# Four weight chunks of a two-layer decoder kernel split by Pool's queue one layer ahead, first convolution taps on ScalarE, statistics over wider pieces

## The chip, the cores and the metric

One NeuronCore of a Trainium2 chip runs the whole kernel. Its engines are TensorE (PE in the rows), VectorE (DVE), ScalarE (ACT), GpSimd (POOL, here called Pool) and SyncE (SP), each with an instruction queue of its own that it works off in order; an instruction that waits holds up what is queued behind it. DMAs are issued from the queues of SP and Pool here. The metric is the device time of one execution, in microseconds (us), the median of several runs.

## The reference

Two residual layers over x of 512 tokens by 1024 channels, in float32. Cut to what matters:

```python
def fox_moba_layer(x, norm_g, w_in, b_f, ..., w_out):           # layer 0
    proj = rms_norm(x, norm_g) @ w_in       # FoX q,k,v | forget logits | MoBA q,k,v | gate
    out_a = fox_attention(qa, ka, va, logf) # 8 heads: logits + c[q] - c[k], causal, softmax
    out_b = moba_attention(qb, kb, vb)      # 8 heads: top-3 key blocks + own causal block
    mix = jnp.concatenate([out_a, out_b], axis=2).reshape(B, S, MIX_WIDTH)
    return x + (mix * jax.nn.silu(gate)) @ w_out

def conformer_conv_layer(x, norm_g, w_in, conv_w, conv_b, ln_g, ln_b, w_out):   # layer 1
    val, glu_gate, z = jnp.split(rms_norm(x, norm_g) @ w_in, 3, axis=-1)
    u = val * jax.nn.sigmoid(glu_gate)
    u = causal_depthwise_conv(u, conv_w) + conv_b        # 31 taps along the tokens
    u = jax.nn.silu(layer_norm(u, ln_g, ln_b)) * jax.nn.silu(z)
    return x + u @ w_out
```

## The kernel before

**Weights.** All weights come in 36 chunks of 1 MB (128 partitions by 2048 numbers). To keep the accuracy of float32 each matrix is written as a rounded part `hi` and a remainder `lo`, and a product is three matmuls (L361 for the token-major form, L370 to L372 for the channel-major one). Chunks 0 to 15 are layer 0's input projection, 16 to 19 its output projection, 20 to 27 the value and gate halves of layer 1's GLU, 28 to 31 its z path, 32 to 35 its output projection (used in the order 33, 34, 32, 35).

**How a chunk becomes two parts.** SP fetches it into one of two staging buffers `wst` (L152). `split_w` makes `hi` as a rounded copy on ScalarE (L173) or by a casting DMA issued by Pool (L169, chunks in `CAST`). The remainder is a subtraction on VectorE or Pool (L177), or, for the chunks in `DMAS` (all from 20 on), a copy of the negated chunk on ScalarE (L175) to which a DMA issued by Pool adds the chunk itself (L179). The parts live in rings: `whi` and `wlo` with two buffers each ("main"), `wx` with four, and for chunk 32 ("late") a tile of its own, with its `hi` fetched later by Pool (L1051). `ahead` calls the split of the next chunk and the fetch of one more, so a staging buffer that is not yet read through holds up the fetches behind it on SP.

**Layer 0.** The dense work is a generator of 56 units over chunks 0 to 15; the attention of eight pairs of heads (four MoBA, then four FoX) advances it with `advance`, so that dense matmuls stand between the attention's. For FoX, Pool adds bias and mask to each tile's row of biases (L518, 32 tiles, two `cb` buffers), VectorE adds that to the scores and takes row maxima (L522), ScalarE makes the exponentials `p` (L523), TensorE transposes them (L526) and multiplies them with the values (L603) in PSUM bank "o", and VectorE divides into the slot of `ot` (L608). The slots 0 to 3 of `ot` belong to the four FoX pairs. Pool also computes the reciprocal roots of q and k (L396).

**Layer 1.** For each of eight channel tiles TensorE makes value and gate, ScalarE and VectorE make `u`, and the convolution's 31 taps are shared: VectorE does some (L766, accumulating in a PSUM bank `s`; the first tap, L763, goes to a tile `first` in SBUF), ScalarE makes products `tm` of the others (L775, six buffers) and Pool adds them up in `pacc` (L776). L783 adds both sums. Then TensorE transposes (L796), VectorE takes statistics (L798) and ScalarE copies to `ctok` (L799). The last two channel tiles, 6 and 7, go through in two halves of 256 tokens. `norm_stats` joins the statistics (L903, L904) and Pool takes the reciprocal root `lnr` (L905); `norm_cols` (L911) normalises `ctok`, TensorE transposes it back (L922), ScalarE (L928) and VectorE (L933) make the product with z, and L936 and L939 split it for the last matmuls.

**What sets the order.** A scheduler orders each engine's queue from the program and its own estimates, except the last stretch from the transposes of channel tile 6 on: there PE, DVE, ACT and POOL have the order written out by hand, with tables saying how many convolution steps stand between the others.

## Time and profile before

| | |
|---|---|
| median of 3 runs | 522.47 us (522.46 to 522.81) |
| the profiled execution | 522.39 us, of it 520.6 us span |
| TensorE busy | 503.7 us, 97% of the span |
| VectorE busy | 373.0 us, 72% |
| ScalarE busy | 329.1 us, 63% |
| Pool busy | 232.6 us, 45% |
| chain that ended last | PE 70%, DMA 8%, POOL 7%, ACT 6%, DVE 4%, issue 3% |

A row of the profile names an engine, a line of the kernel and what is written from what. Shares of busy time are means over stages: layer 0's projections and attention up to about 256 us, its output projection up to about 282, layer 1's projections with the convolution up to about 440, the convolution's end with the normalisation up to about 490, and the last matmuls. The chain of waits is followed back from the last instruction through what released each step.

### The profile page before, as it was taken

To read this page: it belongs to the slowest core of one execution; us is meant where nothing else is said; L and a number is where in the kernel's file an instruction comes from. 1 tells how busy PE (TensorE), PEld (TensorE's weight loads), DVE (VectorE), ACT (ScalarE), POOL (GpSimd) and SP (SyncE) were. 2 spreads that over 40 slices of the span, in tenths; PEclk is the share of its full clock that TensorE was granted. 3 is DMA by queue.
4 is the path that set the end of the run, shared out by engine and by line. 5 is a ranking of instruction groups with operands and counts; after the bars stand their busy time and mean duration, and the time that the engine had idled before them with its cause. 6 is when DMAs were issued, how large, how long until landed. Compare 5 with 4: busy or idle time off the path is not lost.

```text
span 520.6 us, 9754 instructions
## 1 busy us (share of the span) xinstructions
PE 503.7 (97%) x3694; PEld 459.9 (88%) x3694; DVE 373.0 (72%) x788; ACT 329.1 (63%) x668; POOL 232.6 (45%) x255
## 2 busy tenths in 40 slices
PE   8999999999999999999999999999999999769997
PEld 4999998987889988788789999999999888548997
DVE  7745677676465577596685256999999997868741
ACT  4945678777645775576384735998676765377230
POOL 5264852020422233223101113879988985687200
PEclk9999999999999999999999999999999999989999
DMA  8742222302122242402219668488999799962111
GB/s 293 318 145 81 84 81 83 102 24 83 61 102 94 82 111 99 144 14 108 102 52 395 130 205 242 82 211 286 235 306 259 212 270 305 262 170 105 41 51 42
DMA packets 16566, 79.05 MB, mean 152 GB/s; under 512 B 1988, under 2 KB 4352, under 8 KB 8712
## 3 DMA queue, kind: packets, MB, share of 16 engines
q1 hardware_dynamic: 12632, 51.08, 27.1%
q0 software_dynamic: 3744, 27.26, 22.0%
q8 instruction: 29, 0.48, 0.4%
q10 hardware_dynamic: 144, 0.09, 0.1%
q14 instruction: 17, 0.14, 0.1%
HBM read 50.07 MB, written 2.14 MB: 100 GB/s over the span
## 4 chain that ended last, share of the span: by engine, by line
PE 70%; DMA 8%; POOL 7%; ACT 6%; DVE 4%; issue 3%; SPq 0%; POOLq 0%; ACTq 0%
PE mm L361 29%; POOL pacc L776 6%; PE mm L370 6%; PE mm L371 6%; PE mm L372 6%; DMA wst<-in_w_dram 5%; PE st L361 4%; PE o L603 3%; PE tp L526 3%; PE o L361 2%; PE s L510 2%; PE s L512 2%; DMA wlo<-wst 1%; DMA xt<-in_xt_dram 1%; PE s L361 1%
## 5 line engine op out<-in xcount | busy, mean ns | idle before, releaser
L776 POOL TENSOR_TENSOR pacc<-pacc,tm 128x256 f32<-128x256 f32 (+1 forms) x125 | 120.7, 986 | 15.8 <-ACT tm L775 10.1
L766 DVE SCALAR_TENSOR_TENSOR s<-u,parts,s 128x256 f32<-128x256 f32 (+1 forms) x211 | 108.1, 569 | 0.5
L361 PE MATMUL mm<-wlo,hhi 128*128 128x256 f32 (+1 forms) x352 | 98.7, 287 | 0.8 <-DVE wlo L177 0.5
L361 PE MATMUL mm<-whi,hhi 128*128 128x256 f32 (+1 forms) x352 | 98.4, 287 | 0.0
L361 PE MATMUL mm<-whi,hlo 128*128 128x256 f32 (+1 forms) x352 | 98.3, 286 | 0.0
L775 ACT ACTIVATE tm<-u,parts 128x256 f32<-128x256 f32 (+1 forms) x125 | 66.2, 571 | 14.5 <-POOL pacc L776 14.0
L361 PEld LDWEIGHTS mm<-wlo,hhi 128*128 128x128 f32 x352 | 65.8, 190 | 2.0 <-DVE wlo L177 0.8
L361 PEld LDWEIGHTS mm<-whi,hhi 128*128 128x128 f32 x352 | 65.6, 189 | 0.7 <-issue 0.2
L361 PEld LDWEIGHTS mm<-whi,hlo 128*128 128x128 f32 x352 | 65.9, 190 | 0.2
L177 POOL TENSOR_TENSOR wlo<-wst,whi 128x512 fp32r<-128x512 f32 (+1 forms) x22 | 31.0, 1423 | 57.4 <-ACT whi L173 57.4
L173 ACT ACTIVATE whi<-wst 128x512 fp32r<-128x512 f32 (+2 forms) x77 | 49.4, 707 | 5.9 <-DMA wst<-in_w_dram 2.7
L518 POOL TENSOR_TENSOR cb<-cb,mask 128x128 f32<-128x128 f32 x32 | 15.5, 490 | 80.7 <-DVE nm L522 46.2
L523 ACT ACTIVATE p<-p,nm 128x128 f32<-128x128 f32 (+3 forms) x64 | 35.7, 559 | 24.1 <-DVE nm L522 23.6
L177 DVE TENSOR_TENSOR wlo<-wst,whi 128x512 fp32r<-128x512 f32 (+1 forms) x50 | 39.8, 830 | 9.0 <-PE o L361 7.1
L370 PE MATMUL mm<-nhi,wx 128*128 128x256 f32 (+1 forms) x104 | 33.0, 318 | 0.0
L371 PE MATMUL mm<-nlo,wx 128*128 128x256 f32 (+1 forms) x104 | 32.2, 309 | 0.0
L372 PE MATMUL mm<-nhi,wx 128*128 128x256 f32 (+1 forms) x104 | 31.9, 307 | 0.0
L371 PE MATMUL mm<-nlo,whi 128*128 128x256 f32 (+1 forms) x104 | 31.8, 307 | 0.0
L372 PE MATMUL mm<-nhi,wlo 128*128 128x256 f32 (+1 forms) x104 | 31.7, 306 | 0.0
L370 PE MATMUL mm<-nhi,whi 128*128 128x256 f32 (+1 forms) x104 | 31.7, 307 | 0.0
L526 PE MATMUL tp<-identf,p 128*128 128x128 f32 x160 | 28.4, 275 | 1.1 <-ACT p L523 0.7
L396 POOL TENSOR_TENSOR rq<-vq,mhalf 128x16 f32<-128x16 f32 x8 | 26.2, 3272 | 6.2 <-DVE vq L394 6.1
(292 smaller groups left out, 1436.3 us busy)
## 6 DMA issues: line engine op xcount, KB each, us to landing
wst<-in_w_dram SPq DMA_DIRECT2D x33, 1024.0 KB, 5.0
wx<-wst POOLq DMA_DIRECT2D x13, 1024.0 KB, 7.2
wlo<-wst POOLq DMA_DIRECT2D x8, 1024.0 KB, 8.4
whi<-wst POOLq DMA_DIRECT2D x3, 1024.0 KB, 4.5
wst<-in_w_dram SPq DMA_DIRECT2D x2, 1040.0 KB
xs<-in_x_dram SPq DMA_DIRECT2D x4, 512.0 KB, 10.3
...
```

The costliest lines, as they stand in the source:

```text
L173: A.activation(hi[:, ks], st[:, ks], AF.Copy)
L177: (V if eng is G and parts == 4 and k % 4 and V0 else eng).tensor_tensor(lo[:, ks], st[:, ks], hi[:, ks].bitcast(F32), op=ALU.subtract)
L361: T.matmul(po, a[:, k, ts], b[:, k, :n], start=first and i == 0, stop=last and i == len(prods) - 1)
L370: T.matmul(po, whi[:, k, cs], a, start=k == 0, stop=False)
L371: T.matmul(po, whi[:, k, cs], b, start=False, stop=False)
L372: T.matmul(po, wlo[:, k, cs], a, start=False, stop=k == KC - 1)
L396: G.tensor_tensor(r, v, mhalf[:, :16].rearrange("p (t h) -> p t h", t=NT), op=ALU.pow)
L523: A.activation(p[:, :w], p[:, :w], AF.Exp, bias=nm, scale=-1.0, accum_out=sm[:, h, t:t + 1])
L526: T.transpose(tp[:, j * P:(j + 1) * P], p[:, j * P:(j + 1) * P], identf)
L766: V.scalar_tensor_tensor(acc[:, o], v, w, first[0][:, :n] if i == 1 else acc[:, o], op0=ALU.mult, op1=ALU.add)
L775: A.activation(tm[:, :n], v, AF.Copy, scale=w)
L776: G.tensor_tensor(pacc[:, o], pacc[:, o], tm[:, :n], op=ALU.add)
```

## The change

Three edits.

**Chunks 30 to 33 (`PRE`) are split in layer 0.** Each is taken in four quarters. For a quarter, Pool's queue issues two DMAs from memory, the plain one into `st` and a casting one into `hi`; in the following step Pool subtracts the one from the other (128 by 512) and issues two DMAs of 256 KB that write both parts to a tile `pre` in device memory. Even quarters use the slots 0 and 1 of `ot` as buffers, odd ones 2 and 3, before the FoX pairs write there. A step is called from `advance` when the count of dense units reaches an entry of `UNITS`, and its first instruction waits for ScalarE's emptying of the newest dense unit (`unit`). In layer 1 SP fetches the finished parts straight into their rings, and neither `wst`, ScalarE nor Pool has to do with these four chunks. All in all 64 DMAs and 16 subtractions are added on Pool's queue in layer 0; four fetches into `wst`, four copies on ScalarE (three L175, one L160), three casting and four accumulating DMAs and one fetch on Pool's queue go from layer 1. Chunks 34 and 35 keep the old way.

**The first tap** is made by ScalarE, with bias and scale, straight into VectorE's PSUM bank. The tile `first` goes.

**Statistics.** For channel tiles 0 to 3 they are taken once, over 512 channels of `ctok`, for 4 and 5 over 256; 6 and 7 stay as they were. So four sets are joined instead of eight.

```diff
-DMAS = (20, 21, 22, 23, 24, 25, 26, 27, 28, 29, 30, 31, 32, 33, 34, 35)
+DMAS = (20, 21, 22, 23, 24, 25, 26, 27, 28, 29, 34, 35)
...
-CAST = (22, 26, 27, 28, 30, 31, 33, 34, 35)
+CAST = (22, 26, 27, 28, 34, 35)
+PRE = range(30, 34)
+UNITS = (22, 24, 25, 26, 27, 28, 29, 30, 31, 32, 34, 36, 38, 40, 42, 43, 45)
...
     def split_w(w, ring, eng, parts, cast):
         st, n = w
-        if ring == "late":
-            lo = l1p[0].tile([P, KC * WC], F32R, tag="gh", name="lo", bufs=1)
-            lo = lo.rearrange("p (k n) -> p k n", k=KC)
-            A.activation(lo, st, AF.Copy, scale=-1.0)
-            G.dma_start(lo.bitcast(F32), st, accum_op=ALU.add)
-            return None, lo
...
     def fetch(i):
-        if i < len(wsrc):
+        if i < len(wsrc) and i not in PRE:
             raw[i] = load_w(*wsrc[i], 4 if i == 0 else 1)
+    pre = {i: dram.tile([2, P, KC * WC], F32, name=f"pre{i}") for i in PRE}
+    def load_part(i, j, x):
+        SY.dma_start(x.bitcast(F32).rearrange("p k n -> p (k n)"), pre[i][j])
+        return x
+    def load_parts(i):
+        if rings[i] == "late":
+            lo = l1p[0].tile([P, KC * WC], F32R, tag="gh", name="lo", bufs=1)
+            return None, load_part(i, 1, lo.rearrange("p (k n) -> p k n", k=KC))
+        pool, tags, bufs, wide = (main, ("whi", "wlo"), 2, WPAD) if rings[i] == "main" else \
+            (l1p[0], ("wx", "wx"), 4, WC)
+        return tuple(load_part(i, j, flat(pool, F32R, tags[j], WC, bufs, wide)) for j in range(2))
     def split(i):
-        if i < len(wsrc):
+        if i in PRE:
+            wts[i] = load_parts(i)
+        elif i < len(wsrc):
             wts[i] = split_w(raw.pop(i), rings[i], SPLIT_ENG(i, nc), APARTS if i in DMAS else 4 if i == 0 or 17 <= i < 24 else WPARTS, i in CAST)
     fetch_xt(0, 2)
...
-            A.activation(raw_t[:, t, :], po[:, :WC], AF.Copy, scale=rinv[:, t:t + 1])
+            unit[0] = A.activation(raw_t[:, t, :], po[:, :WC], AF.Copy, scale=rinv[:, t:t + 1])
...
-            A.activation(e, g, AF.Tanh)
+            unit[0] = A.activation(e, g, AF.Tanh)
+    QC = KC * WC // 4
+    behind = mybir.DependencyInfo(mybir.DependencyClass.Sync, mybir.DependencyReason.DATA)
+    def quarters(place, parts):
+        was = None
+        for n, (i, q) in enumerate(parts + [(None, None)]):
+            mine = []
+            def then(f, *a, **k):
+                with tc.issue_after(mine[-1].ins) if mine else nullcontext():
+                    mine.append(f(*a, **k))
+            if was:
+                i0, q0, st, hi = was
+                then(G.tensor_tensor, st, st, hi, op=ALU.subtract)
+                for j, x in enumerate((hi, st)):
+                    then(G.dma_start, pre[i0][j][:, q0 * QC:(q0 + 1) * QC], x)
+            if i is not None:
+                st, hi = place[:, n % 2 * 2], place[:, n % 2 * 2 + 1]
+                src = w_ap(*wsrc[i], q * KC // 4, KC // 4)
+                then(G.dma_start, st, src)
+                then(G.dma_start, hi.bitcast(F32R), src)
+                was = i, q, st, hi
+            tc.add_manual_dep(mine[0].ins, unit[0].ins.name, behind)
+            yield
+    steps = list(UNITS)
+    presplit = quarters(ot, [(i, q) for i in PRE for q in range(4)])
...
         while done < min(n, 64):
             next(dn, None)
             done += 1
+            if steps and steps[0] <= done:
+                steps.pop(0)
+                next(presplit)
     att = attention()
     total = 0.0
...
-    stats = l1.tile([P, NT, KC, 6], F32, name="stats")
+    stats = l1.tile([P, NT, 4, 6], F32, name="stats")
...
-        first = []
         def vstep(i):
             v, w = tap(i)
             if i == 0:
-                first.append(l1.tile([P, S], F32, tag="first", name="first", bufs=FB))
-                V.tensor_scalar(first[0][:, :n], v, w, cbias[:, ct:ct + 1], op0=ALU.mult,
-                                op1=ALU.add)
+                A.activation(acc[:, o], v, AF.Identity, bias=cbias[:, ct:ct + 1], scale=w)
             else:
-                V.scalar_tensor_tensor(acc[:, o], v, w, first[0][:, :n] if i == 1 else acc[:, o],
-                                       op0=ALU.mult, op1=ALU.add)
+                V.scalar_tensor_tensor(acc[:, o], v, w, acc[:, o], op0=ALU.mult, op1=ALU.add)
         def astep(i):
             v, w = tap(i)
...
         pt = tpbank()
         for t in range(t0, t0 + n):
             last[1] = T.transpose(pt[:, t * P:(t + 1) * P], pacc[:, t * P:(t + 1) * P], identf)
-        for t in range(t0, t0 + n):
-            V.bn_stats(stats[:, t, ct, :], pt[:, t * P:(t + 1) * P])
+        if ct >= KC - NLATE:
+            for t in range(t0, t0 + n):
+                V.bn_stats(stats[:, t, ct - 4, :], pt[:, t * P:(t + 1) * P])
         A.activation(ctok[:, t0:t0 + n, ct * P:(ct + 1) * P],
                      pt[:, t0 * P:(t0 + n) * P].rearrange("p (t c) -> p t c", t=n), AF.Copy)
+        if ct in (3, 5):
+            for t in range(t0, t0 + n):
+                V.bn_stats(stats[:, t, ct // 5, :], ctok[:, t, 4 * (ct // 5) * P:(ct + 1) * P])
     def new_pacc():
         return l1.tile([P, S], F32, tag="pacc", name="pacc", bufs=2)
-    nf, nsp = [18], [17]
+    nsp = [17]
+    nf = [i for i in range(18, len(wsrc)) if i not in PRE]
     def ahead(n):
         while nsp[0] < n:
             split(nsp[0])
             nsp[0] += 1
-            fetch(nf[0])
-            nf[0] += 1
+            if nf:
+                fetch(nf.pop(0))
     with tc.issue_after(his[-2].ins):
         ahead(18)
...
             if p == C34:
                 hi = main.tile([P, KC, WC], F32R, tag="big", name="hi", bufs=3)
-                G.dma_start(hi.rearrange("p k n -> p (k n)"), w_ap(*wsrc[32], 0, KC))
-                wts[32] = hi, wts[32][1]
+                wts[32] = load_part(32, 0, hi), wts[32][1]
             if p in (1, 2):
                 ng_t(0, p + 1)
             for (c, t), po in zip(units, banks):
```

Three places of the order. First Pool's queue among the additions of bias and mask of the FoX heads (`cb`), before and then with the change (L518 becomes L535, L177 becomes L174, the steps' instructions carry L658):

```order
L518 TENSOR_TENSOR cb<-cb,mask 128x128 x7
L396 TENSOR_TENSOR rq<-vq,mhalf 128x16
L518 TENSOR_TENSOR cb<-cb,mask 128x128 x3
L177 TENSOR_TENSOR wlo<-wst,whi 128x512 x2
L518 TENSOR_TENSOR cb<-cb,mask 128x128 x10
```

With the change Pool's queue has at this place:

```order
L174 TENSOR_TENSOR wlo<-wst,whi 128x512
L658 DMA pre_99<-ot 128x512
L658 DMA ot<-in_w_dram 128x512 x2
L535 TENSOR_TENSOR cb<-cb,mask 128x128 x3
L658 TENSOR_TENSOR ot<-ot 128x512
L658 DMA pre_99<-ot 128x512 x2
```

Between the additions there now stand loads of quarters into `ot`, the subtraction and the stores to `pre_99`, which is chunk 33.

Second Pool's queue in the last stretch, around the reciprocal root `lnr` of the first half of the tokens, before and with the change (L776 becomes L823, L905 becomes L957, L169 and L179 become L166 and L176):

```order
L776 TENSOR_TENSOR pacc<-pacc,tm 128x256 x14
L169 DMA wx<-wst 128x2048
L776 TENSOR_TENSOR pacc<-pacc,tm 128x256
L179 DMA wx<-wst 128x2048
L905 TENSOR_TENSOR lnr<-lnv,mhalf 128x2
L776 TENSOR_TENSOR pacc<-pacc,tm 128x256 x8
```

With the change Pool's queue has around the root:

```order
L823 TENSOR_TENSOR pacc<-pacc,tm 128x256 x7
L166 DMA wx<-wst 128x2048
L823 TENSOR_TENSOR pacc<-pacc,tm 128x256 x2
L176 DMA wx<-wst 128x2048
L823 TENSOR_TENSOR pacc<-pacc,tm 128x256 x3
L957 TENSOR_TENSOR lnr<-lnv,mhalf 128x2
L823 TENSOR_TENSOR pacc<-pacc,tm 128x256 x26
```

The two DMAs of the last chunk stood straight before the root, one addition apart; now five additions stand between the casting DMA and the root, and the fetch that these DMAs wait for stands further ahead on SP's queue (there the sixteen fetches into `wst` become twelve, then the fetches of `pre`).

Third ScalarE's queue at the same place, before and with the change (`u_3251` and `u_3335` are channel tile 6, `u_3337` is channel tile 7, L812 is the new first tap):

```order
L772 ACTIVATE pacc<-u_3251,parts 128x256
L775 ACTIVATE tm<-u_3251,parts 128x256 x3
L175 ACTIVATE wx<-wst 128x2048
L799 ACTIVATE ctok<-tp 128x2x128
L1007 ACTIVATE zs<-mm 128x512
L775 ACTIVATE tm<-u_3251,parts 128x256 x7
L928 ACTIVATE c<-tp,parts 128x256 x2
```

With the change ScalarE's queue has there:

```order
L819 ACTIVATE pacc<-u_3335,parts 128x256
L822 ACTIVATE tm<-u_3335,parts 128x256 x3
L812 ACTIVATE s<-u_3335,parts 128x256
L847 ACTIVATE ctok<-tp 128x2x128
L1059 ACTIVATE zs<-mm 128x512
L822 ACTIVATE tm<-u_3335,parts 128x256 x7
L812 ACTIVATE s<-u_3337,parts 128x256
L980 ACTIVATE c<-tp,parts 128x256 x2
```

The copy of the last chunk (`wx<-wst`) moved ahead of the first of these rows, and two first taps came in, the second behind seven products. On VectorE, with the change, the taps before the normalisation (L963) read them:

```order
L955 BN_AGGR mv<-stats 128x2 x2
L956 TENSOR_SCALAR lnv<-mv 128x2
L814 SCALAR_TENSOR_TENSOR s<-u_3335,parts,s 128x256 x2
L814 SCALAR_TENSOR_TENSOR s<-u_3337,parts,s 128x256
L814 SCALAR_TENSOR_TENSOR s<-u_3335,parts,s 128x256
L963 TENSOR_SCALAR ctok<-ctok,mv,lnr 128x512 x4
```

Before, three taps of channel tile 6 and the first two of channel tile 7 stood there, all VectorE's own; now there are four taps, each on a first tap that ScalarE has made.

## Rows read from the trace of the kernel before

**Rows 1.** Busy us by stretch: length, engines (PE, PEld, DVE, ACT, POOL), clock, DMA, GB/s.

```profile
144.00:200.00 56.00, 56.00 (x449) 52.47 (x448) 35.54 (x71) 34.80 (x80) 14.90 (x18) 1.00 0.29 95
...
282.00:440.00 158.00, 157.57 (x1213) 151.42 (x1212) 132.58 (x267) 109.59 (x173) 105.49 (x111) 1.00 0.84 234
440.00:490.00 50.00, 40.90 (x259) 35.42 (x258) 37.58 (x91) 28.46 (x65) 35.52 (x47) 0.97 0.57 158
```

**Rows 2.** Chain of waits, 165 to 256 us, by line.

```profile
by line: PE mm L361 23.8%; PE mm L370 15.3%; PE mm L371 15.0%; PE mm L372 14.9%; PE tp L526 8.5%; PE o L603 7.9%; PE s L510 5.8%; PE s L512 5.4%; PE st L483 1.6%; PE st L495 1.4%; PE tp L543 0.4%
```

**Rows 3.** Waits, 165 to 256 us: us in total, times, longest us.

```profile
ACT p L523 <- DVE nm L522: 14.8, 10, 3.1
```

**Rows 4.** TensorE's timeline: start, us, work [idle before, what ended it].

```profile
444.35 0.44 PE L796 MATMUL tp<-identf,pacc 128*128 128x128 f32 x2 [1.48 <-DVE pacc L783]
...
452.04 0.41 PE L796 MATMUL tp<-identf,pacc 128*128 128x128 f32 x2 [1.74 <-DVE pacc L783]
...
460.50 0.30 PE L922 MATMUL tp<-identf,ctok 128*128 128x128 f32 x1 [3.92 <-DVE ctok L911]
```

**Rows 5.** Busy time by stretch, four microseconds after the third stop.

```profile
461.00:465.00 4.00, 3.73 (x13) 3.13 (x13) 3.94 (x7) 1.42 (x3) 3.67 (x5) 0.57 1.00 199
```

**Rows 6.** Chain of waits, 440 to 490 us: start us, us, what.

```profile
436.68 7.72 DMA wlo<-wst
...
444.53 10.91 DMA wst<-in_w_dram
...
455.53 1.91 ACT wx L175
...
457.74 0.87 POOL wx L179
458.61 0.76 POOL lnr L905
...
459.40 1.83 DVE ctok L911 x2
```

**Rows 7.** Timelines of VectorE and ScalarE in the tail.

```profile
443.87 0.42 DVE L783 TENSOR_TENSOR pacc<-s,pacc 128x256 f32<-128x256 f32 x1 [3.68 <-POOL pacc L776]
...
451.46 0.42 DVE L783 TENSOR_TENSOR pacc<-s,pacc 128x256 f32<-128x256 f32 x1
...
453.52 0.17 DVE L904 TENSOR_SCALAR lnv<-mv 128x2 f32<-128x2 f32 x1
...
458.09 2.89 ACT L775 ACTIVATE tm<-u,parts 128x256 f32<-128x256 f32 x7
```

**Rows 8.** Groups by shape, 282 to 521: count | busy, mean ns | idle.

```profile
L763 DVE TENSOR_SCALAR first<-u,parts 128x512 f32<-128x512 f32 x4 | 5.1, 1287 | 0.0
...
L175 ACT ACTIVATE wx<-wst 128x2048 fp32r<-128x2048 f32 x7 | 13.4, 1909 | 10.6 <-DMA wst<-in_w_dram 6.9 <-PE mm L372 1.9 <-issue 1.9
...
L776 POOL TENSOR_TENSOR pacc<-pacc,tm 128x256 f32<-128x256 f32 x85 | 66.9, 793 | 14.6 <-ACT tm L775 10.1 <-ACT pacc L772 0.2
...
L169 POOL DMA_DIRECT2D whi<-wst x3 | 1.8, 614 | 5.0 <-DMA wst<-in_w_dram 4.3 <-PE mm L372 0.6
```

**Rows 9.** The same view of Pool, 80 to 256 us.

```profile
L177 POOL TENSOR_TENSOR wlo<-wst,whi 128x512 fp32r<-128x512 f32 x8 | 11.1, 1409 | 40.8 <-ACT whi L173 40.8
```

**Rows 10.** Pool's busy time, sum of 80:120, 120:144, 144:200 and 200:256 us.

```profile
sum 176.00, POOL 44.96; mean POOL 11.24
```

**Rows 11.** Timelines of Pool's additions and of VectorE's reading them.

```profile
176.38 0.43 POOL L518 TENSOR_TENSOR cb<-cb,mask 128x128 f32<-128x128 f32 x1 [2.57 <-DVE nm L522]
...
204.99 0.42 POOL L518 TENSOR_TENSOR cb<-cb,mask 128x128 f32<-128x128 f32 x1
...
179.00 0.42 DVE L522 CUSTOM_DVE_ANT_0 p<-s,cb 128x256 f32<-128x256 f32 x1 [0.52 <-PE mm L361]
...
207.02 0.27 DVE L522 CUSTOM_DVE_ANT_0 p<-s,cb 128x128 f32<-128x128 f32 x1
```

**Rows 12.** Pool's timeline, the longest issue of an accumulating DMA.

```profile
290.52 1.05 POOL L179 DMA_DIRECT2D wlo<-wst  x1 [14.87 <-ACT jk L710]
```

5 lines of the change are left out of this document (3 added, 2 removed).

## Prediction

> **What bounds the kernel now.** I read the busy shares by stretch first [rows 1]. TensorE is busy 56.00 of 56 us in the attention stretch 144 to 200 and 157.57 of 158 us from 282 to 440; from 440 to 490 it is busy only 40.90 of 50. So until 440 us nothing that makes another engine faster can gain; what can be gained lies in the 9 us of 440 to 490, and what can be lost lies wherever TensorE is full now.
>
> The chain of the attention stretch is made of TensorE lines alone [rows 2]: dense matmuls (L361, L370 to L372) with the attention's own matmuls between them. Softmax steps are late there without cost: ScalarE waited ten times, up to 3.1 us, for VectorE's row maximum [rows 3], and TensorE still stood at full.
>
> The tail is another matter. TensorE's three long stops there [rows 4]: 1.48 us before 444.35, 1.74 before 452.04, 3.92 before 460.50. They mean that TensorE was ready at 442.87, 450.30 and 456.58. After the third stop the granted clock falls to the lower of its two levels (1.2 GHz): from 461 to 465 its mean is 0.57 of full [rows 5], which costs (1 − 0.57) × 4 = 1.7 us. The mean of 0.97 over all 50 us [rows 1] is this one fall (1.7 of 50 us is 0.03), so the shorter stops cost no clock.
>
> The chain says who made them late [rows 6]. Pool's queue stands behind the copy and accumulation of chunk 34 (436.68, 7.72 us); the fetch of chunk 35 follows (444.53, 10.91 us, slower than usual); ScalarE splits it (455.53, 1.91); Pool issues the accumulating DMA (457.74, 0.87) and only then computes the reciprocal root (458.61, 0.76) which VectorE's normalisation waits for (459.40). The root's input was ready at 453.52 + 0.17 = 453.69 [rows 7]. So some 5 us of the third stop is a queue of Pool standing behind a weight chunk that has nothing to do with the normalisation.
>
> **The change, part by part.**
>
> *The tail's fetches.* Chunks 30 to 33 need no fetch into the staging buffers, so chunks 34 and 35 follow 29 there directly, in the places that 30 and 31 had. Pool's waits for 34 and 35 and ScalarE's for 35 go; four copies on ScalarE of 1.909 us each [rows 8] go as well. What is late next, stage by stage:
> - Channel tile 6. Before, VectorE's last addition came at 443.87 after 3.68 us of waiting for Pool [rows 7], which stood behind chunk 34. Without that it is ready at about 439, ahead of TensorE's 442.87: the stop of 1.48 goes.
> - Channel tile 7. TensorE is then ready at 450.30 − 1.48 = 448.82. VectorE's last addition was at 451.46 [rows 7] with 3.68 us of waiting ahead of it that go, and some first-tap work between that goes too; against this its new first tap waits for ScalarE, which comes behind the copy of chunk 34. I take 448.4, so the stop of 1.74 goes too; bounds 0 to 1 us of it left.
> - Normalisation. Before, the root's input came 453.69 − 452.04 = 1.65 us after the last transposes began; now these begin at 448.82, so it comes at 450.5, and the root (0.76, and up to one of Pool's additions of 0.793 ahead of it [rows 8]) at about 451.6. Now a new wait decides: VectorE runs the normalisation behind a tap of channel tile 7, second half, whose first tap ScalarE makes only after its seven products (2.89 us for seven [rows 7]). ScalarE empties the transposes and z from 449.3 and makes seven products to about 453.3. The first tap writes into PSUM, which no product of the trace does; I take 0.5 us, a little over a product's 2.89 / 7 = 0.41, with 0.41 and 1.0 as bounds: 453.8. Two short taps on VectorE follow, together some 0.9, so the normalisation starts about 454.7 instead of 459.40. That is 4.7 us earlier. TensorE, ready at 456.58 − 3.22 = 453.36, gets its first transpose 1.1 us after the normalisation's start as before, at 455.8: the stop is about 2.4 us instead of 3.92.
> - After it, the second half of the convolution is bound by Pool's additions. They begin after the root, 451.6 instead of 459.4, so they move by no less than TensorE does. I let the rest move along by 4.7 and add 0.3 for a clock that falls for less time or not at all: **−5.0**. Bounds: −2.5 if the new wait on ScalarE comes 2 us later than worked out; −8 if the root decides (7 us earlier) and the clock stays at full.
>
> *Less work on VectorE and a little more on ScalarE.* The four wide first taps that go were 1.287 us each [rows 8], 5.1 together; with the eight narrow ones, the faster second taps and the fewer statistics I reckon with up to twice that. Nearly all lies between 282 and 440, where TensorE is at 157.57 of 158: **0** outside the tail. If TensorE were not the cover, it would be worth 5 to 10. ScalarE gains twelve taps of 0.4 to 1.0 and loses four copies, 7.6 us: 0.
>
> *Layer 0: sixteen steps on Pool.* Each step adds a subtraction, 1.409 us by the row of the same shape [rows 9], and four DMA issues on Pool's queue, 0.614 each by the copy's row [rows 8], the longest of any kind 1.05 [rows 12]: 1.41 + 4 × 0.61 = 3.9 us, at most 5.6. Sixteen steps make 62 us. Between 80 and 256 us Pool is busy 44.96 of 176 [rows 10], so there is room in the sum; the question is what is queued behind a step. Eleven of the sixteen lie among the 32 additions of bias and mask that VectorE's row maxima wait for. Pool has each of these done some time ahead: the one that starts at 204.99 is read at 207.02, 1.6 us after its end [rows 11]. For the one that starts at 176.38 the distance is 2.2. These are the first and the last of eleven; the mean of the eleven is 3.1. A step of 3.9 us ahead of one makes it late by about 0.8 us; eleven times that is 8.8 us if every one goes through to TensorE. How much does? In this stretch ten waits of 14.8 us on the same path [rows 3] went through with nothing. I take a sixth: **+1.5**, bounds 0 and +5. In this stand also: each step's first instruction waits for ScalarE to empty a dense unit, which blocks Pool's additions behind it when the unit is late; the reciprocal roots of q on Pool come up to 1 us later; and VectorE's division of the first FoX pair's output stands behind the last step that uses the same buffer, so its PSUM bank comes free for the next pair's product with the values some ten tiles later than before (0 to 2 us). Traffic of 16.8 MB is added where the DMA engines are at a share of 0.29 [rows 1], which can lengthen loads of bias tiles.
>
> A rule speaks against DMAs issued by Pool here. The trace shows issues of 0.614 us in the mean [rows 8] in a stretch where VectorE was busy 132.58 of 158 us [rows 1]; the longest was 1.05 [rows 12]. The Trainium skill, "SBUF — State Buffer", section "A bandwidth-pool intuition that's wrong (but worth ruling out)", has a Pool-issued DMA of about 620 ns alone take about 3100 ns beside a VectorE copy, since Pool can't write descriptors while VectorE holds the port they share. An estimate by that page's figure would make a step 1.4 + 4 × 3.1 = 13.8 us and sixteen of them 221, more than Pool's idle time. The trace so far leans against it.
>
> *Loads from memory.* SP fetches finished parts, 2 MB a chunk instead of 1. Both are fetched as soon as their buffers are free; before, the rounded copy was fetched then, and the other part followed ScalarE's copy of 1.909 us. So they come no later unless they slow each other down: the longest transfer of 1 MB in the tail is 10.91 us [rows 6], and TensorE had no stop for these chunks up to 440 [rows 1]. Covered, **0**; if not, up to 2 us at the start of the last z products, which the bound of −2.5 takes in.
>
> **Sum.** The profiled execution of before took 522.39 us (the median of the runs is 522.47, so the sum carries over as it is): 522.4 − 5.0 + 1.5 + 0 = 518.9, with the 0.1 to the median **519.0 us**. Its own bounds: 517 to 521.3.
>
> **Rivals.**
> - *Pool's queue becomes the bound in layer 0 (slower).* If TensorE has no slack left behind the softmax, all eleven delays of 0.8 go through: 522.4 − 5 + 8.8 = 526.2. It ends above before by 1 us from a loss of 0.55 us for each step on. For it: TensorE is full there and its order is fixed. Against it: ten waits of up to 3.1 us that cost nothing [rows 3].
> - *ScalarE's first taps eat the gain of the tail.* If the normalisation stands behind the tap and that behind products that wait for Pool's additions (0.793 each [rows 8] against 0.41 a product), the tail gains 2: 522.4 − 2 + 1.5 = 521.9, no change that can be told.
> - *Layer 0 is free and the tail gains whole.* 522.4 − 8 = 514.4. For it: Pool is idle 131 of 176 us [rows 10], and the root alone could come 7 us earlier. Against it: the new wait on ScalarE.
> - *The issues are held up by VectorE.* By the longest issue of the trace [rows 12] a step is 1.41 + 4 × 1.05 = 5.6 us and late by 2.5, eleven times 27; a sixth of it through, +4.6: 522.0. By the figure of the Trainium skill's page "SBUF — State Buffer" it would be far more, with Pool full.
> - The change does what it says in the order of the program: the steps stand on Pool's queue and the fetches are gone from SP's.
>
> **How the numbers follow.** The measurement can tell about 0.2%, 1.0 us. Chances: forecast 0.57, Pool bound 0.16, first taps 0.14, more 0.10, held-up issues 0.03. Faster than 521.4: 0.55 of the forecast, 0.10 of more, 0.02 of the first taps, 0.67; within: 0.02 + 0.11 + 0.03 = 0.16; slower than 523.5: 0.16 + 0.01 = 0.17. The range from 514.5 to 524.5 leaves out half of "more" and most of "Pool bound", under 0.2.
>
> **What would show it.** Stops before the transposes of channel tiles 6 and 7 gone, the third at 2 to 2.5 us, the root on Pool straight after its input; TensorE still at 56 of 56 from 144 to 200, and at the same work at 256 as before within 2 us; Pool issues at 0.6 in layer 0. Wrong would be: the start of layer 1 more than 4 us late, a stop for weights between 400 and 440, or a normalisation that starts as late as before.

## The result, and the profile after

The changed kernel is slower: 527.26 us in the median (527.02 to 529.31) against 522.64 (522.46 to 523.87) of the kernel before on the same chip, a ratio of 1.0092 with a 95% interval of 1.0065 to 1.0118. Forecast were 519.0 us and a range up to 524.5. The profiled execution took 527.13 us, of it a span of 525.4 (before 520.6).

The stretches that answer to [rows 1], and the two between them; the columns are those of that group:

```profile
120.00:144.00 24.00, 23.17 (x157) 17.95 (x157) 16.30 (x41) 15.42 (x39) 15.00 (x17) 1.00 0.58 168
144.00:200.00 56.00, 55.66 (x452) 52.14 (x451) 33.13 (x66) 34.96 (x79) 36.02 (x45) 1.00 0.66 202
200.00:256.00 56.00, 52.99 (x263) 41.43 (x261) 38.54 (x79) 31.71 (x72) 33.57 (x45) 0.97 0.57 169
256.00:282.00 26.00, 24.58 (x149) 18.34 (x149) 19.39 (x45) 15.38 (x36) 3.44 (x5) 0.93 0.23 79
282.00:440.00 158.00, 157.97 (x1249) 153.49 (x1248) 124.18 (x234) 110.70 (x190) 102.61 (x107) 1.00 0.79 237
440.00:490.00 50.00, 45.15 (x265) 38.86 (x264) 39.42 (x95) 30.53 (x65) 32.62 (x43) 0.97 0.44 126
```

From 440 to 490 TensorE is now busy 45.15 us where it was 40.90 [rows 1]: the tail did get shorter. The loss is in layer 0. In 200 to 256 the same row of before reads

```profile
200.00:256.00 56.00, 56.00 (x290) 43.65 (x289) 40.45 (x85) 32.90 (x77) 18.41 (x22) 1.00 0.31 104
```

so 56.00 − 52.99 = 3.0 us of TensorE are gone there, and the clock of 0.97 costs another 0.03 × 56 = 1.7; in 256 to 282 the clock of 0.93 (before 1.00) costs 0.07 × 26 = 1.8.

A finer measure counts TensorE's matmul records in both traces and subtracts the starts of records with the same number; some records may be missing, so 0.2 us mean nothing. By it the changed kernel lies behind by 0.5 us at 119 us, 2.1 at 138, 2.65 from 168 to 198, 3.3 at 232, 7.4 at 248, 9.4 to 9.6 from 289 to 443, and 4.5 from 473 on. **Layer 0 loses 9.4 us (forecast 1.5), the tail gives back 4.9 (forecast 5.0).** Below, "behind at 294" and "at the end" are this measure. Up to 3.4 of the 9.4 is the granted clock: 1.7 in 200 to 256 and 1.8 in 256 to 282, by the two sums above, which go by rounded means.

Where layer 0 stands shows in the chain of waits. From 110 to 126 us (start us, us, what):

```profile
111.45 7.09 DMA ot<-in_w_dram
...
118.68 1.29 POOL ot L658
119.97 0.52 POOL pre L658
...
120.51 1.31 POOL wlo L174
121.82 0.52 POOL jp L265
...
122.36 0.43 DVE tri L471
122.79 0.60 DVE p L539
...
124.77 0.82 ACT p L540 x2
...
125.64 0.44 PE tp L543 x2
```

Read it from the top: Pool's step stands for the load that the step before it issued; behind it in Pool's queue wait the remainder of a weight chunk (L174) and the index row `jp` (L265), for `jp` VectorE's `tri`, for that the exponentials, and for these TensorE. The other place is the first FoX division (197.4 us in the kernel before), in the same view from 225 us on:

```profile
223.46 6.45 DMA ot<-in_w_dram
...
230.05 1.77 POOL ot L658
231.81 1.06 POOL pre L658 x2
...
234.80 4.89 issue
239.69 0.06 DVE ot L625
```

and on VectorE's and TensorE's timelines (start us, us, work, and in brackets the idle time before and what ended it):

```profile
239.69 0.69 DVE L625 TENSOR_TENSOR ot<-o,rb 128x512 f32<-128x512 f32 x1 [6.39 <-issue]
...
240.44 2.69 PE L620 MATMUL o<-pt,v 128*64 128x512 f32 x8 [3.01 <-DVE ot L625]
```

The step at 230.05 came after 6.45 us of load, its stores out of slot 0 were issued at 231.81, and VectorE stood 6.39 us until that slot could be written; TensorE stood 3.01. The row names no releaser ("issue"); that it was the second store follows from the stores' times to landing from 225 to 250 us, the longest of them 7.3 (issued at about 232.3, landed at 239.6):

```profile
L658 POOL DMA_DIRECT2D pre<-ot x4: 544/570/578, 231.8 to 244.0; - x4
...
DMA to landing us min/median/max: 2.6/3.6/7.3
```

The granted clock fell to the lower of its two levels (1.2 GHz) right after this stop, to a mean of 0.66 from 240 to 245, and once more at 270 to 275 (0.68):

```profile
240.00:245.00 5.00, 4.56 (x19) 1.86 (x19) 4.87 (x12) 3.37 (x8) 3.23 (x4) 0.66 0.30 113
245.00:270.00 25.00, 24.04 (x122) 18.31 (x122) 16.62 (x40) 10.45 (x29) 7.76 (x10) 1.00 0.25 85
270.00:275.00 5.00, 4.54 (x19) 2.17 (x21) 4.58 (x9) 5.00 (x11) 0.00 (x0) 0.68 0.01 3
```

Pool's steps by group from 40 to 290 us (count | busy us, mean ns | idle us before them and what ended it), and from the page's DMA issues their KB and median us from issue to landing:

```profile
L658 POOL TENSOR_TENSOR ot<-ot 128x512 f32<-128x512 f32 x16 | 24.7, 1547 | 60.1 <-DMA ot<-in_w_dram 51.0 <-ACT v L438 5.8 <-ACT p L540 3.3
...
L658 POOL DMA_DIRECT2D pre<-ot x32 | 18.3, 574 | 0.0
L658 POOL DMA_DIRECT2D ot<-in_w_dram x32 | 17.7, 559 | 0.3 <-ACT v L438 0.3
```

```profile
ot<-in_w_dram POOLq DMA_DIRECT2D x32, 256.0 KB, 6.0
pre<-ot POOLq DMA_DIRECT2D x32, 256.0 KB, 3.5
```

A step's own work is 1.55 + 2 × 0.574 + 2 × 0.559 = 3.8 us, as forecast (3.9). Beside it Pool stood 60.1 / 16 = 3.8 us a step, 51.0 of the 60.1 for loads. The forecast has no term for that.

The tail, on TensorE's timeline, and the chain from 440 to 490 us:

```profile
458.69 0.41 PE L843 MATMUL tp<-identf,pacc 128*128 128x128 f32 x2 [0.80 <-DVE pacc L830]
465.47 0.30 PE L974 MATMUL tp<-identf,ctok 128*128 128x128 f32 x1 [2.24 <-DVE ctok L963]
```

```profile
460.54 2.79 ACT tm L822 x7
463.32 0.47 ACT s L812
463.81 0.88 DVE s L814 x2
464.69 1.50 DVE ctok L963 x2
```

Against [rows 4] the stop of channel tile 6 is gone, that of 7 is 0.80 (was 1.74), the third 2.24 (was 3.92). The wait that decides now is the one that was named: seven products, the first tap, two taps on VectorE, the normalisation.

### The profile page after: what moved, and what is told of

Same layout as the page of the kernel before. It is cut to its first block, busy times and chain, and to the rows that moved or that the text cites. A ratio compares the mean times of both kernels' runs of the same rounds, so it can differ in the third digit from the quotient of the medians.

```text
span 525.4 us, 9834 instructions
## 1 busy us (share of the span) xinstructions
PE 508.6 (97%) x3694; PEld 461.4 (88%) x3694; DVE 365.5 (70%) x760; ACT 328.0 (62%) x676; POOL 283.6 (54%) x327
## 3 DMA queue, kind: packets, MB, share of 16 engines
q0 software_dynamic: 8736, 35.66, 27.2%
HBM read 61.61 MB, written 10.53 MB: 137 GB/s over the span
## 4 chain that ended last, share of the span: by engine, by line
PE 72%; DMA 10%; DVE 7%; POOL 4%; issue 3%; ACT 2%; SPq 1%; DVEq 0%; ACTq 0%; POOLq 0%
PE mm L375 28%; PE mm L384 5%; PE mm L385 5%; PE st L375 5%; PE mm L386 5%; DMA ot<-in_w_dram 4%; DMA rb<-sdram 3%; PE st L384 3%; PE st L385 3%; PE st L386 2%; PE o L620 2%; PE o L375 2%; PE tp L543 2%; DVE s L814 2%; PE s L375 2%
## 5 line engine op out<-in xcount | busy, mean ns | idle before, releaser
L823 POOL TENSOR_TENSOR pacc<-pacc,tm 128x256 f32<-128x256 f32 (+1 forms) x125 | 118.1, 956 | 26.0 <-ACT tm L822 14.8
L814 DVE SCALAR_TENSOR_TENSOR s<-u,parts,s 128x256 f32<-128x256 f32 (+1 forms) x223 | 115.8, 575 | 7.6 <-ACT s L812 5.7
L658 POOL TENSOR_TENSOR ot<-ot 128x512 f32<-128x512 f32 x16 | 24.7, 1547 | 60.1 <-DMA ot<-in_w_dram 51.0
L174 DVE TENSOR_TENSOR wlo<-wst,whi 128x512 fp32r<-128x512 f32 (+1 forms) x50 | 41.1, 856 | 11.2 <-PE o L375 7.1
L174 POOL TENSOR_TENSOR wlo<-wst,whi 128x512 fp32r<-128x512 f32 (+1 forms) x22 | 30.7, 1402 | 18.5 <-ACT whi L170 18.5
L620 PE MATMUL o<-pt,v 128*64 128x512 f32 (+3 forms) x128 | 24.0, 492 | 3.0 <-DVE ot L625 3.0
```

The lines of the kernel that those rows point to most:

```text
L174: (V if eng is G and parts == 4 and k % 4 and V0 else eng).tensor_tensor(lo[:, ks], st[:, ks], hi[:, ks].bitcast(F32), op=ALU.subtract)
L620: mm = T.matmul(po[h * HD:(h + 1) * HD, kt * P:], vt[grp][:, kt, hd * HD:(hd + 1) * HD], pts[h][:, kt * (PTS + P):kt * PTS + S], start=kt ...
L814: V.scalar_tensor_tensor(acc[:, o], v, w, acc[:, o], op0=ALU.mult, op1=ALU.add)
L823: G.tensor_tensor(pacc[:, o], pacc[:, o], tm[:, :n], op=ALU.add)
```

## The experiments

Each kernel is the changed one but for the edit shown, or (called "chunks alone") with the first taps and the statistics of before. Ratios are to the kernel before on the same chip. "Of it clock" is (1 − mean granted clock) × 294 us of the same trace, so what falls of the clock cost at most up to 294 us; the kernel before has none there. Each trace is one execution, and the runs of one kernel spread by several us (f6: 523.87 to 530.87), so 1 to 2 us between two traces are weak evidence by themselves.

| kernel | median us | ratio, 95% interval | behind at 294 | of it clock | at the end |
|---|---|---|---|---|---|
| the change | 527.26 | 1.0092 [1.0065, 1.0118] | 9.5 | 3.4 | 4.5 |
| e1 taps and statistics alone | 525.29 | 1.0063 [1.0042, 1.0083] | 0 | 0 | 1.5 |
| e2 chunks alone | 526.02 | 1.0074 [1.0055, 1.0093] | 9.4 | 3.4 | 3.7 |
| e3 plain copies by SP | 531.13 | 1.0174 [1.0135, 1.0213] | 16.1 | 5.1 | 10.8 |
| f1 chunks alone, no wait for units | 527.06 | 1.0086 [1.0058, 1.0113] | 10.2 | 1.7 | 4.4 |
| f6 chunks alone, steps from unit 10 | 525.74 | 1.0064 [1.0030, 1.0098] | 8.4 | 1.7 | 2.7 |
| e7 slot pairs exchanged | 526.26 | 1.0060 [1.0030, 1.0090] | 10.7 | 1.7 | 5.6 |
| f8 chunks alone, last one in eighths | 535.59 | 1.0233 [1.0197, 1.0269] | 19.0 | 5.1 | 13.3 |
| g1 chunks alone, other buffers at the end | 526.82 | 1.0080 [1.0053, 1.0107] | 11.2 | 3.4 | 5.4 |
| e9 two chunks | 529.57 | 1.0134 [1.0103, 1.0164] | 3.5 | 0 | 6.6 |
| e8 three chunks | 523.45 | 1.0013 [0.9993, 1.0032] | 4.0 | 0 | 1.1 |
| f9 three chunks and statistics | 518.76 | 0.9925 [0.9907, 0.9943] | 2.6 | 0 | −3.9 |
| f10 three chunks and first taps | 519.40 | 0.9942 [0.9926, 0.9958] | 2.3 | 0 | −3.2 |
| **f7 three chunks alone** | **518.83** | 0.9925 [0.9893, 0.9956] | 2.3 | 0 | −5.0 |
| g2 three chunks alone, every second unit | 525.33 | 1.0051 [1.0023, 1.0078] | 11.1 | 3.4 | 3.8 |
| g3 chunks alone, short loads | 518.28 | 0.9920 [0.9895, 0.9945] | 1.8 | 0 | −5.5 |
| h1 chunks alone, next load first | 525.19 | 1.0050 [1.0030, 1.0070] | 9.3 | 0 | 2.0 |
| h2 three chunks alone, next load first | 524.23 | 1.0013 [0.9982, 1.0043] | 9.0 | 0 | 1.7 |
| i1 chunks alone, copies by Pool | 522.37 | 0.9990 [0.9969, 1.0011] | 6.0 | 0 | 0.2 |

### Which part costs

e1 has no chunk split ahead; e2 has the chunk part alone:

```diff
-PRE = range(30, 34)      # e1
+PRE = range(0)
...
-                A.activation(acc[:, o], v, AF.Identity, bias=cbias[:, ct:ct + 1], scale=w)      # e2
+                first.append(l1.tile([P, S], F32, tag="first", name="first", bufs=1))
+                V.tensor_scalar(first[0][:, :n], v, w, cbias[:, ct:ct + 1], op0=ALU.mult,
+                                op1=ALU.add)
...
```

> The first taps on ScalarE and the wide statistics alone; all chunks are split in layer 1 as before. Theory: the 9.4 us that the changed kernel lost came in layer 0 from the steps on Pool's queue, so layer 0 is as before and only the tail can move, by little since chunks 34 and 35 come late as before: 521 to 523 us. Rival, the new waits on ScalarE's first taps cost time of their own: above 524.

> The four chunks split in layer 0 alone; first taps and statistics as before. Theory: layer 0 loses the same 9 us up to the start of layer 1 and the tail gains 4 to 6 from the earlier chunks, so 526 to 528 us. Rival, the first taps made half of the gain of the tail: 529 to 530. Rival, the first taps spoilt the tail: 523 to 525.

e1 leaves layer 0 alone and loses in the tail; e2 loses the whole 9.4 us of layer 0, with the same two falls of the clock, and gains 5.7 in the tail. So the loss belongs to the sixteen steps, and the first taps are no help: without the fetches gone, the stop of channel tile 6 is 3.81 us (1.48 in [rows 4]).

### What in the steps costs

e3 makes both parts plain copies from memory to memory by SP's queue; the rounding, the remainder and the wait for the dense unit are left out.

```diff
-            if was:
...
-            tc.add_manual_dep(mine[0].ins, unit[0].ins.name, behind)
...
+            for j in range(2):
+                then(SY.dma_start, pre[i][j][:, q * QC:(q + 1) * QC], src)
```

> The changed kernel, but the parts of the four chunks are plain copies of the chunk, made from memory to memory by DMAs of SP's queue at the same steps, so that Pool's subtractions, its DMA issues and the buffers in the output slots are left out while as many bytes are read and written. What is left out: the rounding and the remainder of four chunks. Theory, Pool's queue and the buffers make the loss: layer 0 loses 0 to 2 us, the tail gains 5, so 517.5 to 519.5 us. Rival, the traffic makes the loss: 525 to 527.

Without that wait the first copies were issued at 10.81 us (the change's first loads at 79), so they didn't stand at the change's steps, though that was expected of them. They came ahead of weight fetches on SP's in-order queue; TensorE was 9.5 us behind at 66 us, waiting for weights (4.8 us for ScalarE's `whi`). This says what early copies on SP cost, nothing on Pool's steps.

f1 takes away the wait for the newest dense unit; f6 begins at unit 10, a step every one and a half units:

```diff
-            tc.add_manual_dep(mine[0].ins, unit[0].ins.name, behind)      # f1
...
-UNITS = (22, 24, 25, 26, 27, 28, 29, 30, 31, 32, 34, 36, 38, 40, 42, 43, 45)      # f6
+UNITS = (10, 11, 13, 14, 16, 17, 19, 20, 22, 23, 25, 26, 28, 29, 31, 32, 34)
```

> The four chunks split in layer 0, first taps and statistics as before, and the steps don't wait for a dense unit any more; the scheduler then puts them earlier: nine additions of bias and mask stand ahead of the last store instead of twenty-four, and VectorE's first FoX division stands behind 12 softmax tiles instead of 21 (before: 11). Theory: no stop at the first FoX pair (4.0) nor behind it (2.5); of the 9.4 us about 2 to 3 stay and the tail gains 5.8: 518.5 to 520 us. Rival, steps any place cost the same: 526. Rival, earlier loads collide with the fetches of layer 0's weights: above 524 with stops of TensorE for weights before 120 us.

> As the last one, but with the wait for the dense unit kept and the steps called from the 10th dense unit on, one each one and a half units; the division stands behind 13 softmax tiles, the last store behind 15 additions. Theory: as the last, 518.5 to 520.5 us. Rival, collisions with the weights' fetches: above 524.

Neither helps: 10.2 and 8.4 us behind instead of 9.4. The loss only moves forward: f1 is 8.3 us behind at 173 us, f6 6.9, the change 2.65.

e7 exchanges the pairs of slots, g1 puts the last two quarters into an idle tile so that the last store out of slot 0 is that of the thirteenth quarter, f8 takes the last chunk in eighths in slots 2 and 3 (twenty steps, from unit 20 on), so that the first division is free early:

```diff
-                st, hi = place[:, n % 2 * 2], place[:, n % 2 * 2 + 1]
+                st, hi = place[:, 2 - n % 2 * 2], place[:, 3 - n % 2 * 2]      # e7
...
+                st, hi = ((spare if n > 13 else place)[:, n % 2 * 2 + j] for j in range(2))      # g1
...
+                if m == 1:
+                    st, hi = (place[:, 2 + j, n % 2 * WC:(n % 2 + 1) * WC] for j in range(2))      # f8
...
```

> The changed kernel with the two buffer pairs exchanged: even quarters in output slots 2 and 3, odd ones in 0 and 1, so that the last store out of slot 0 is that of the last quarter, one step later. Theory, the division of the first FoX pair waits for that store and the bank for the next pair with it: the wait grows by a step of some 6 to 10 us, TensorE stops 5 to 9 us longer there, 532 to 536 us. Rival, the loss is the steps' own time on Pool's queue: within 1 us of the changed kernel, 527.

> Four chunks split in layer 0, first taps and statistics as before, all sixteen steps at the same places of Pool's queue, but the last two quarters are staged in the tile of MoBA's values, which nobody reads any more, so that the last store out of slot 0 is that of the thirteenth quarter; VectorE's first FoX division stands behind 16 softmax tiles instead of 21. If the division's wait is the loss: the 4.0 us at the division and most of the 2.5 behind it go, layer 0 loses 3 to 4, 519 to 520.5 us. If Pool's standing is the loss: 525 to 527.

> All four chunks split in layer 0, first taps and statistics as before, but the last chunk in eight half quarters that use output slots 2 and 3 alone, so that slot 0 and 1 are free after the third chunk: twenty steps instead of sixteen, and VectorE's first FoX division stands behind 12 softmax tiles instead of 21. Theory, the division's wait for the last store out of its slot makes 6 to 7 of the 9.4 us that layer 0 loses: layer 0 loses 3 to 4, the tail gains 5.8 to 7.3, 518.5 to 520.5 us. Rival, the last four quarters cost that wherever their buffers are, because Pool stands: 525 to 527 us.

All three are still 10.7 to 19 us behind at 294. e7 kept the stop: TensorE stood 3.4 us for a division. In f8 the first division (210.27) waited for no store, but a later one did for 4.7 us. In g1 the first division (215.02) still waited 2.7 us for a store, but TensorE didn't stop for it; its longest wait after 200 us became

```profile
PE s L527 <- DVE nm L539: 2.2, 1, 2.2
```

in the view of waits (us in total, times, longest us). So the division's wait, the most striking row of the changed kernel's trace, isn't all that the loss hangs on: where TensorE no longer stops for it, other late pieces show in its place.

### How many chunks

e8, e9 and f7 take three, two and again three chunks (f7 chunks alone); f9 and f10 give e8 the old first taps and the old statistics.

```diff
-PRE = range(30, 34)
-UNITS = (22, 24, 25, 26, 27, 28, 29, 30, 31, 32, 34, 36, 38, 40, 42, 43, 45)
+PRE = range(30, 33)      # e8, f7, f9, f10
+UNITS = (22, 24, 25, 26, 27, 28, 29, 30, 31, 32, 34, 36, 38)
...
+PRE = range(30, 32)      # e9
+UNITS = (22, 24, 25, 26, 27, 28, 29, 30, 31)
```

> Only chunks 30 and 31 split in layer 0, in eight quarters; 32 and 33 as before. The last store out of the output slots then comes before the first FoX pair. Theory: the loss of 4 us at the first FoX pair's division and the 2.5 us behind it go, about 2 us near 95 to 136 stay, and the tail gains 3 to 5: 519.5 to 521.5 us. Rival, each step costs its share of the 9.4 us: 4.7 lost, 4 gained, 523 us.

> The whole change with three chunks instead of four (chunk 33 as before). Against three chunks with the old first taps and statistics, 518.8 us. Theory, first taps on ScalarE cost the tail a wait and a fallen clock: 1 to 2.5 us slower than that, 520 to 521.5 us. Rival, they only cost where chunk 35 is late, as in the run without any chunk moved: 518 to 519.

> Chunks 30 to 32 only, twelve quarters, first taps and statistics as before; the division stands behind 11 softmax tiles as before the change. Theory: the stop at the first FoX pair and what follows it go, layer 0 loses 2 to 3.5 us; the tail gains 3 to 5 if the order of layer 1 brings no new stop: 520 to 522 us. Rival, every step costs its share: 12/16 of 9.4 is 7, 524 us.

> Three chunks, first taps as before, the wide statistics. Theory, the statistics are off the path, since VectorE waits for Pool in the tail anyway: within 0.5 us of three chunks alone, 518.3 to 519.3. Rival, fewer instructions on VectorE bring the normalisation forward: 1 us faster.

> Three chunks, first taps on ScalarE, old statistics. Theory, this is what costs in the tail: as the whole change with three chunks, 520 to 521.5 us. Rival: 518 to 519.

With the last four steps gone layer 0 loses 2.3 us instead of 9.4, though the twelve that stay stand for loads almost as long each (46.4 / 12 = 3.9 us). Of these 7.1 us up to 3.4 are the two falls of the clock, which f7 hasn't; the page's row of the clock in 40 slices of the span, tenths of full speed (9 is 0.90 or more), first of the change, then of f7:

```profile
PEclk9999999999999999998989999999999999989999
```

```profile
PEclk9999999999999999999999999999999999999999
```

The cost isn't so much a step; it hangs on what is late behind it. f7 is faster than both kernels, 0.7% under before, and its tail gains 7.3 (its ten runs go from 517.75 to 523.05 us, and the trace is of the fastest): all stops on TensorE from 436 to 480 us over 0.5 us are

```profile
451.70 0.41 PE L848 MATMUL tp<-identf,pacc 128*128 128x128 f32 x2 [0.77 <-DVE pacc L835]
...
460.32 0.38 PE L375 MATMUL st<-whi,u 128*128 128x256 f32 x1 [0.98 <-ACT u L989]
461.55 0.52 PE L375 MATMUL st<-whi,u 128*128 128x256 f32 x2 [0.73 <-DVE u L992]
471.89 0.50 PE L375 MATMUL st<-whi,u 128*128 128x256 f32 x2 [0.62 <-DVE u L992]
```

and the clock of 440 to 490 is 1.00. It was 0.97 in the kernel before, and that fall cost 1.7 us [rows 5], so up to 1.7 of the 7.3 is the clock. Statistics over wider pieces change nothing that can be told (f9 against f7: 518.76 and 518.83). First taps on ScalarE leave a tail gain of 5.5 instead of 7.3 in the trace (f10), though the medians differ by 0.6 only, which is inside their intervals; both together leave 2.9 (e8, median 4.0 above f10's). There a late fetch of the last chunk and the first taps meet: that fetch was issued at 439.41 us in e8 and at 438.47 in f9, which has no such taps and loses nothing by it, but at 432.91 in f10. The chain of e8 in the tail:

```profile
439.41 10.87 DMA wst<-in_w_dram
...
452.93 1.20 ACT tm L822 x3
454.12 0.47 ACT s L812
454.61 0.94 DVE s L814 x3
...
455.79 0.43 DVE pacc L830
```

ScalarE's first tap comes behind the copy of that chunk, and VectorE's last addition behind the tap: TensorE stood 3.96 us before 456.35, and the clock of 455 to 460 was 0.50. e9 lost little in layer 0 but got a new stop of 5.0 us at 417 us, where ScalarE had stood 7.3 us for a weight chunk ahead of the sigmoids that TensorE needed, and the clock of 420 to 430 fell to a mean of 0.66; that is layer 1's order, not the steps.

### Transfers, or standing for them

g3 cuts the loads to 64 of 512 columns (seven eighths of the four chunks are left out) and clears the slots once at the start; h1 and h2 issue the next step's loads ahead of the subtraction, h2 with three chunks; g2 takes three chunks with a step every second unit; i1 makes the parts by DMAs of Pool's queue from memory to memory, with no buffer, no subtraction and no waiting for a transfer (rounding and remainder left out). It reads and writes as many bytes of device memory as the change (61.61 and 10.53 MB in both pages), but with half as many transfers: Pool's queue moved 27.27 MB in all, in the change 35.66.

```diff
+                then(G.dma_start, st[:, :64], src)      # g3
+                then(G.dma_start, hi[:, :64].bitcast(F32R), src)
...
+    V.memset(ot[:, :4], 0.0)      # g3
...
+            old, was = was, None      # h1, h2: the subtraction and stores of `old` behind the loads
...
+UNITS = (18, 20, 22, 24, 26, 28, 30, 32, 34, 36, 38, 40, 42)      # g2
...
+            for j in range(2):      # i1
+                then(G.dma_start, pre[i][j][:, q * QC:(q + 1) * QC], src)
```

> Four chunks, first taps and statistics as before; each quarter's loads fetch only 64 of 512 columns, so they land in some 2 to 3 us instead of 6; subtraction and stores are whole. What is left out: seven eighths of four chunks. If Pool's standing for loads is the loss: layer 0 loses at most 4, 519 to 521 us, with Pool's wait for loads down from 48 us to under 15. If the division's wait is it: that shrinks too as far as the store lands sooner, but a stop of 2 us or more stays: 522 to 525.

> Four chunks, first taps and statistics as before, same bytes, steps and issues, but in each step the next quarter's two loads are issued ahead of the subtraction and the stores of the last one. If Pool's standing for its loads is the loss of layer 0: the wait falls from 48 us to about 20 and the loss from 9.4 to 3 to 5, 519.5 to 522 us. If the bytes are: 525 to 527. The buffers are released later now, so the stores must have landed before a load is issued, which can bring a new wait on Pool's queue: then 524 and more with that wait in Pool's rows.

> The same with three chunks, to be held against three chunks with the loads last (518.8 us). Pool's standing: the 2.3 us of layer 0 fall to about 1, 517.5 to 518.5. The bytes, or a new wait for the stores: 518.8 or slower.

> Three chunks, first taps and statistics as before, steps called every second dense unit from the 18th on. If Pool's standing for loads makes the 2.3 us that three chunks still lose in layer 0, they fall to about 1: 517 to 518.5 us. If not, as three chunks before, 518.8, or worse where steps meet the weights' subtractions near 60 us.

> The chunk part alone (old first taps and statistics), with the same four chunks, the same sixteen steps each behind its unit, and the same bytes read, written in layer 0 and read back in layer 1; but each step is two DMAs of Pool's queue straight from memory to memory, 256 KB each, with no buffer between, so that nothing on Pool waits for a transfer and no subtraction is there. Left out: the parts' rounding and the remainder; both parts are copies of the weights. Theory (Pool stood for transfers, and what is queued behind it was late): Pool's waits for loads and stores are gone, what is left is some 1.2 us of issues a step; layer 0 loses at most 2 us against the kernel before, the tail gives back about 5, and the time is 518 to 519.5 us. Rival (the bytes themselves: 8 MB more traffic in layer 0 makes the transfers that others wait for later, whoever stands): layer 0 still loses 7 to 10 us with Pool free, and the time is 525 to 527 us. Something between, with layer 0 at 4 to 6 us, would leave both at work.

Pool's groups from 40 to 290 us, first g3, then h1, then i1:

```profile
L658 POOL TENSOR_TENSOR ot<-ot 128x512 f32<-128x512 f32 x16 | 22.0, 1375 | 30.3 <-DMA ot<-in_w_dram 20.3 <-ACT v L438 5.8 <-ACT p L540 4.3
```

```profile
L658 POOL TENSOR_TENSOR ot<-ot 128x512 f32<-128x512 f32 x16 | 21.3, 1330 | 0.9 <-DMA ot<-in_w_dram 0.8
...
L658 POOL DMA_DIRECT2D ot<-in_w_dram x32 | 18.0, 566 | 45.1 <-DMA pre<-ot 26.4 <-ACT p L540 9.4 <-ACT v L438 6.3
```

```profile
L658 POOL DMA_DIRECT2D pre<-in_w_dram x32 | 17.3, 544 | 53.8 <-ACT v L438 31.2 <-ACT qk L403 22.5
```

g3 keeps all sixteen steps, subtractions, stores, issues and waits for units, and is only 1.8 us behind. Even these aren't the steps': it is 1.7 us behind at 50 us already, 30 us ahead of its first load (80.6), since VectorE spends 1.76 us at 7.88 on clearing the slots. So the steps with short loads cost nothing that can be told: what costs is the loads and what stands or is slowed for them, not Pool's work.

h1 takes the standing away from the subtraction, and it comes back nearly whole at the loads, which now wait for the stores of the step before and for units: 45.1 us. Its 9.3 us are another loss than the change's: no fall of the clock is among them, and it is behind by 2.9 us at 122 and by 7.6 at 198. Between these its chain holds a 128 KB load of SP's queue (`rb`) of 7.19 us at 162.76, issued beside Pool's loads; the same kind of load took 2.95 at 137.29.

How long Pool stands doesn't give the loss. With three chunks f7 stood 46.4 us and lost 2.3. In g2 Pool stood 46.3 us before subtractions, 12.1 of it for late dense units (`qk`), and TensorE was 10 us behind at 173 us already. h2 stood 37.1 us (1.4 before subtractions, 35.7 before loads) and lost 9.0, with a `rb` load of 6.89 us on its chain. With three chunks too the place of the steps decides.

i1 came out between: 6.0 us behind, 3.6 of them by 122 us and 0.6 after 229, with a single wait for a bias addition (2.1 us). That is as much as the change and e2 lose when the clock is taken off (9.4 − 3.4 = 6.0); whether that is chance isn't shown. Its chain from 108 to 120 us holds no step of Pool, but the small transfers of a MoBA pair, of 4 and 128 KB:

```profile
108.70 4.28 DMA sdram<-rt
...
113.54 3.38 DMA rb<-sdram
```

In g3 the two took 2.62 and 3.09 at about the same place. So traffic can reach TensorE without Pool's standing. But i1 isn't the change with the standing taken out: its steps stand elsewhere in Pool's queue and wait 53.8 us for dense units, and in the change the chain at this place is the load shown above.

## Why the prediction was wrong

**The step that failed is layer 0: +1.5 us was taken, +5 was its bound, +9.4 came.** By its parts:
- *A step's price.* 3.9 us forecast, 3.8 measured. The subtraction was 1.55 us (1.41 taken from [rows 9]), the issues 0.56 to 0.57. The rival of issues held up by VectorE fell: the 64 issues had means of 0.574 and 0.559 us. The Trainium skill's 3100 ns beside a VectorE copy ("SBUF — State Buffer", "A bandwidth-pool intuition that's wrong (but worth ruling out)") is seen nowhere in these runs: the longest issue on Pool's queue in any of them was 1.25 us. VectorE's costliest group beside the steps was a subtraction (`wlo`, 21.2 us from 80 to 256), so the page's case, a copy, is hardly tested here.
- *What was left out.* The step was priced as work; its in-order queue also stands for the transfer that the step before issued. That is 3.8 us a step, as much again, and no term of the sum had it. The loads took 6.0 us from issue to landing. By the fit of the Trainium skill ("DMA: Bandwidth & Descriptors", "Anatomy of one DMA — SWDGE (gpsimd) path") 256 KB would make an estimate of 2.6 us; the rows say over twice that. Shortened loads (g3: 3.6 us, 30.3 us of standing) cut the loss to 1.8, of which 1.7 came before the first step. The prediction did ask what is queued behind a step, but into its sum went only the additions, late by 0.8 us each.
- *How much goes through.* A sixth was taken because ten waits of ScalarE had cost nothing [rows 3]. VectorE now waited seven times for the additions from 144 to 256 us (us in total, times, longest); before, no such wait stands in that view:

```profile
DVE p L539 <- POOL cb L535: 7.7, 7, 2.6
```

So these waits came near the 8.8 us of lateness that were reckoned. But the loss doesn't go with it: f1 has 1.5 us of these waits at a loss of 10.2. The larger pieces came by other rows of the same queue: `wlo` and `jp` at 118 to 123 us, and the store that the division needed. The share of a sixth had no row of these behind it.
- *The division.* Named at 0 to 2 us; VectorE stood 6.39 and TensorE 3.01. Yet g1 and f8 show that the loss doesn't hang on it alone.
- *The clock.* Two falls, to means of 0.66 and 0.68 of full speed over five us, added 1.7 and 0.32 × 5 = 1.6 us. No term for it stood in layer 0.
- *Traffic.* "Can lengthen loads of bias tiles" was said and priced at nothing. Bias tiles took 4.8 us from issue to landing (80 to 256 us; before 3.5), the 128 KB loads `rb` for the divisions 6.2 (before 3.0), and i1, h1 and h2 show such transfers on the chain. But in g3 the 128 KB took 6.0 as well at a loss of 1.8 us, and in i1 2.9 at a loss of 6.0: it depends on which of them the chain goes through, and slower transfers alone don't make the 9.4.

How the 6.0 us that the clock doesn't explain divide between standing and traffic is **not settled**: g3 takes away much of both, i1 keeps the bytes but in half as many transfers and with another order of Pool's queue, and f7 stands 3.9 us a step at a loss of 2.3. What is shown is that the loss comes with the steps (e1, e2), that their work isn't it (g3), that the wait of the division isn't all of it (f8, g1), and that the last four steps make the difference between 2.3 and 9.4, up to 3.4 of it by the clock (f7, e2). One of the prediction's own signs of being wrong came: layer 1 began more than 4 us late.

**The tail was right, in size and in mechanism:** −5.0 forecast, −4.9 measured. The stop before tile 7 was taken as 0 (bound 1) and was 0.80. The first tap into PSUM took 0.56 us (0.5 taken); the root on Pool came straight behind its input (459.96 + 0.17, root at 460.21); the normalisation started at 464.60, which less the 9.4 of layer 0 is 455.2 (454.7 forecast); the stop was 2.24 (2.4). Only the 0.3 for a kinder clock didn't come: the mean of 440 to 490 stayed at 0.97. That VectorE's and ScalarE's saved work counts nothing before 440 held (157.97 of 158 us busy), as did the free loads from memory: TensorE had no stop for them. The "some 5 us of the third stop" is misread, though without effect on the sum: 4.9 us is how late the root was (458.61 − 453.69), and the stop itself was 3.92.

**Rivals.** "Pool's queue becomes the bound" (526.2, chance 0.16) came nearest in place and size; its mechanism, eleven additions late by a step's work, is only part of what the runs show. "First taps eat the gain" may be half true: in the traces they cost the tail 1.8 us (f7 against f10) and 0.8 (e2 against the change). In the medians it is 0.6 and 1.2 us, inside the intervals, so that leaving them out is worth more isn't shown.
